# Summing expert outputs into tokens by accumulating indirect reads, and ending the last expert in its own rows

## The chip, the cores and the metric

The kernel runs on one core of one Trainium2 chip. The metric is the device time of one execution in microseconds (us). The engines are called as the profile calls them: PE (TensorE), PEld (its weight loads), DVE (VectorE), ACT (ScalarE), POOL (GpSimd) and SP (SyncE, which issues DMAs). Indirect DMAs, which gather or scatter rows by a column of indices, are issued by POOL.

## The reference

A two-layer encoder over 512 tokens of 1024 features in float32. Layer 0 is neighbourhood attention and a dense SwiGLU, layer 1 is multi-head latent attention and a top-2-of-8 expert SwiGLU; a final RMS norm follows. The change touches the part from the experts on:

```python
def _moe(h, w_router, w_gu, w_down):
    hf = h.reshape(B * S, D)
    probs = jax.nn.softmax((hf @ w_router).astype(jnp.float32), axis=-1)
    vals, idx = lax.top_k(probs, TOP_K)
    wts = vals / jnp.sum(vals, axis=-1, keepdims=True)
    combine = jnp.sum(jax.nn.one_hot(idx, N_EXPERTS, dtype=jnp.float32) * wts[..., None], axis=1)
    y = jnp.zeros_like(hf)
    for e in range(N_EXPERTS):
        y = y + combine[:, e:e + 1] * _swiglu(hf, w_gu[e], w_down[e])
    ...
x = x + g_f[:, None, :] * f      # f is the result of _moe, g_f one row of 1024 gates
return _rmsnorm(x) * final_norm
```

So every token gets two expert rows, each times a weight of its own, the sum times a gate row `g_f`, and is then normalised over its 1024 features.

## The kernel before

Float32 products are made in three passes: each operand is split into a high part (`hi`, cast on ACT, L195) and a rest (`lo`, subtracted on DVE, every sixth piece on POOL, L198), and PE adds hi·hi, hi·lo and lo·hi (L1245 to L1247). A weight tile goes by SP's queue from HBM into a raw slot (L168), is split into one of a few hi/lo slots, and is used by PE. The raw slots are a ring: `N_RAWX` = 3 of a pool for this phase, two in `big_raw`, three of `rawp`; SP issues in order and waits for the next slot of the ring to be split.

The experts are walked in 88 steps, 11 for each expert (`steps`, L1396): steps 0 to 6 are gate and up (256 columns of each), 7 and 8 the left half of the down product, 9 and 10 the right half. One step takes two weight tiles ("jobs"). The order of all instructions is as written (`manual_schedule`). The split of a step's weights is written two steps ahead: `emit_to(2 * i + PRE)` opens step i, `emit_to(2 * i + POST)` closes it, and what a step writes between the two stands on ACT and DVE ahead of the split of step i + 2. An expert handles its first 128 rows always; a second block of up to 128 rows is under a branch on the expert's count (`second_block`, L1382), in a narrow form for at most 64 rows (`few`). In the profiled execution the last expert (number 7) takes the second block, so its gate steps are twice as long.

Tokens that chose an expert are gathered by an indirect read of `HT` into `xb0` and `xb1`. A finished expert's rows leave PSUM by an ACT copy (`out_rows`, L1271) and are written to a DRAM table `Y`, unweighted, 256 rows per expert for experts 0 to 6. While expert 7 runs, eight indirect reads of `Y` (for each of four token blocks of 128 the two chosen experts; column `dest`) go through one tile `xb1`, and DVE multiplies each by the token's weight `wm` and the gate row (L1544) and adds it to `x_tok`, the residual in token order (L1545). `x_tok` lies in `big_raw`, and comes back from the DRAM table `XT` at the beginning of expert 7.

Expert 7's own rows don't go by DRAM. They are weighted on DVE (`weigh`), split, and put into token order by PE with a one-hot matrix `oh` (`last_rows`, L1607 to L1617): 16 products of 512 columns for the left half, twice 16 of 256 for the right one. DVE adds each to `x_tok`, ACT sums the squares (L1623). The right half's down product is made in two pieces of 256 columns, for each of the two row blocks. When all is summed, `final_rstd` makes the reciprocal root and DVE scales eight pieces, each stored as it is done (L1604, L1605). `overflow` handles an expert with more than 256 rows; its branch isn't taken.

Of the kernel before, what the change touches and what calls it, by code (L numbers as in the profile page):

```python
# [19 lines left out]
P = 128  # L20
# [20 lines left out]
N_RAWX = 3  # L41
# [17 lines left out]
class Kernel:  # L59
    def __init__(self, ctx, tc, d, dbg=None):  # L60
# [8 lines left out]
        self.Y = self.dram.tile([(NE - 1) * CAP, D], F32, name="Y")  # L69
# [698 lines left out]
    def ffn_phase(self, xT, hH, hL, norm):  # L768
        nc, tc = self.nc, self.tc
        with ExitStack() as es:  # L770
# [17 lines left out]
            for g, (f0, f1) in enumerate(self.ffn_groups()):  # L788
# [201 lines left out]
    def router(self, small, hp, ps_a, ps_b, ps_c, cst):  # L990
# [64 lines left out]
        def rest(R, C, T, idx0, ps_y):  # L1055
# [33 lines left out]
            dest, wm, near = small("dest", 8, dt=I32), small("wm", 8), small("near", 8)  # L1089
# [23 lines left out]
            for n in range(8):  # L1113
                nc.tensor.matmul(ps[:, 32:34], R[:, n].bitcast(F32), W[:, n], start=n == 0, stop=n == 7)
            tab, idx, w_row = small("tab", 32), small("idx", 32, dt=I32), small("w_row", 2)
            V.tensor_scalar(tab, ps[:, 0:32], -1.0, None, op0=OP.add)
            V.tensor_scalar(idx, tab, 0.0, None, op0=OP.max)
            V.tensor_copy(w_row, ps[:, 32:34])
# [6 lines left out]
            self.rt = dict(idx=idx, tab=tab, dest=dest, wm=wm, w=w, r=r, col=col, w_row=w_row)  # L1125
# [4 lines left out]
    def moe_phase(self, xT, oH, oL):  # L1130
        nc, tc, d = self.nc, self.tc, self.d
        with ExitStack() as es:
# [66 lines left out]
            xb1 = st.tile([P, D], F32, name="xb1")  # L1199
            act1 = st.tile([P, 256], F32, name="act1")  # L1200
# [101 lines left out]
            def few_out(e, n, ps):  # L1302
                gs = w2.tile([P, S], F32, name="yo")[0:FEW]
                nc.scalar.copy(gs, ps[FEW:P])
                nc.vector.tensor_add(gs, ps[0:FEW], gs)
                r0 = e * CAP + P
                nc.gpsimd.dma_start(Y[r0:r0 + FEW, n * S:(n + 1) * S], gs)

            def overflow():

                iota, tokid = cst[:, 0:128], cst[:, 128:132]
                with tc.tile_pool(name="over", bufs=1, side="right") as op:
                    C = op.tile([P, 32], F32, name="C")
                    tab2 = [op.tile([P, 2, NE, 2], F32, name=f"tab2{i}") for i in range(2)]
# [60 lines left out]
                for i in range(4):  # L1375
                    for n in range(3):
                        self.square_sum(x_tok, w2, ssq, n, i)
# [57 lines left out]
            ssq = st.tile([P, 6, 4], F32, name="ssq")  # L1435
# [7 lines left out]
            def weigh(cols, ps, b=0):  # L1443

                for b, p in enumerate(ps, b):
                    t = w2.tile([P, S], F32, name="yo")[:, cols]
                    nc.vector.scalar_tensor_tensor(t, p[:, cols], self.rt["w_row"][:, b:b + 1], gf_row[:, n * S:(n + 1) * S][:, cols], op0=OP.mult, op1=OP.mult)  # L1447
                    self.split_piece(yl[:, n, b, 0, cols], yl[:, n, b, 1, cols], t)

            last = NE - 1  # L1450
            for i, (e, s) in enumerate(steps):
# [16 lines left out]
                parts = [ALL] if e < last or s < 9 else HALVES if s == 9 else HALVES[0:1]  # L1468
# [8 lines left out]
                else:  # L1477
                    if g == 0:
                        pys = [ps_y.tile([P, S], F32, name="y", tag="y") for _ in parts]
                        py = pys[0]  # L1480
# [250 lines left out]
```

## Time and profile before

| what | before |
|---|---|
| device time, median of 3 (lowest to highest) | 1646.16 us (1645.68 to 1646.4) |
| profiled execution, its own device time | 1649.19 us |
| its span, first to last instruction | 1647.3 us |
| mean granted clock of TensorE | 0.989 |
| busy share of the span: PE, PEld, DVE, ACT, POOL | 95%, 76%, 67%, 50%, 19% |
| DMA queue of SP, share of 16 engines' span | 54.0% |

The experts begin at about 935 us. PE is busy nearly all the time: of 20 us it works 18 to 20 in every stretch from 960 to 1620 us. From 1300 to 1480 us the DMA engines are also full (share 0.96 to 1.08). The last expert runs from about 1503 us to the end, and after 1620 us the work thins out: a few PE products, DVE and ACT in turn, then the stores.

A row of a timeline reads: start in us, length in us, engine, line of the code, operation, what is written from what, shape, how many; and in brackets how long the engine was idle before it and whose end it waited for.

### The profile page before, as it was taken

The numbers are of one execution on the slowest core, as the hardware profiler recorded it, in microseconds if no ns is written. First come the engines' busy times: TensorE is split into PE (matmuls) and PEld (weight loads), VectorE is DVE, ScalarE is ACT, GpSimd is POOL, SyncE is SP. The second block draws the span as 40 slices with busy tenths as digits, with TensorE's granted clock in tenths as the row PEclk, the third lists the DMA queues.
The fourth block names the chain that finished last, engine by engine and source line by source line (L and its number), as shares of the span: only waits on it lengthen the run. The fifth ranks groups of instructions, "written<-read, shape, count | busy, mean of one in ns | idle before, by whom it ended". The sixth has DMA issues, their size and how long they took to land. (4 is left out here: it accounts for less than half of the span.)

```text
span 1647.3 us, 23092 instructions
## 1 busy us (share of the span) xinstructions
PE 1572.5 (95%) x7909; PEld 1245.2 (76%) x7909; DVE 1107.1 (67%) x1688; ACT 819.9 (50%) x1384; POOL 310.9 (19%) x259
## 2 busy tenths in 40 slices
PE   6899999999999999989999989999999999999996
PEld 4677779888888888856668677778887777777885
DVE  4687855765655434698865668656447888887765
ACT  3455544422222123577663656545436677765442
POOL 0332310002000000021101343112123324233310
PEclk9999999999999999999999989999999999999998
DMA  9545533467544523222112599758568999997751
GB/s 355 186 141 166 169 119 103 146 216 253 194 160 158 193 77 112 74 77 77 52 65 69 182 360 355 256 187 259 175 192 295 334 351 357 345 371 260 262 192 53
DMA packets 241209, 327.38 MB, mean 199 GB/s; under 512 B 9586, under 2 KB 191570, under 8 KB 240404
## 3 DMA queue, kind: packets, MB, share of 16 engines
q1 hardware_dynamic: 231072, 296.19, 54.0%
q0 software_dynamic: 5232, 18.09, 3.0%
q10 hardware_dynamic: 4740, 11.02, 1.8%
q8 instruction: 89, 1.46, 0.4%
q14 instruction: 76, 0.62, 0.1%
HBM read 308.75 MB, written 16.52 MB: 197 GB/s over the span
## 5 line engine op out<-in xcount | busy, mean ns | idle before, releaser
L198 DVE TENSOR_TENSOR lo<-raw,hi 128x1024 fp32r<-128x1024 f32 (+1 forms) x284 | 374.9, 1350 | 92.4 <-ACT hi L195 84.8
L195 ACT CAST hi<-raw 128x1024 fp32r<-128x1024 f32 (+1 forms) x319 | 318.3, 1045 | 225.0 <-PE mm L296 146.3
L296 PE MATMUL mm<-hL,hi 128*128 128x512 f32 x480 | 190.7, 397 | 0.0
L295 PE MATMUL mm<-hH,hi 128*128 128x512 f32 x480 | 190.1, 396 | 0.1
L297 PE MATMUL mm<-hH,lo 128*128 128x512 f32 x480 | 190.1, 396 | 0.0
L1245 PE MATMUL gu<-hi,he 128*128 128x512 f32 x360 | 144.5, 401 | 9.6 <-ACT act L1255 3.9
L198 POOL TENSOR_TENSOR lo<-raw,hi 128x1024 fp32r<-128x1024 f32 x39 | 101.6, 2606 | 236.1 <-ACT hi L195 187.0
L1247 PE MATMUL gu<-hi,he 128*128 128x512 f32 x360 | 141.2, 392 | 0.0
L1246 PE MATMUL gu<-lo,he 128*128 128x512 f32 x360 | 140.8, 391 | 0.0
L225 DVE SCALAR_TENSOR_TENSOR ada_acc<-raw,c_act,ada_acc 128x1024 f32<-128x1024 f32 x70 | 90.4, 1291 | 31.9 <-DMA raw<-in_w_ada_dram 31.3
L295 PEld LDWEIGHTS mm<-hH,hi 128*128 128x128 f32 x480 | 90.4, 188 | 20.9 <-ACT hi L195 0.5
L296 PEld LDWEIGHTS mm<-hL,hi 128*128 128x128 f32 x480 | 90.3, 188 | 19.9 <-issue 1.0
L297 PEld LDWEIGHTS mm<-hH,lo 128*128 128x128 f32 x480 | 90.4, 188 | 19.2 <-issue 0.2
L1245 PEld LDWEIGHTS gu<-hi,he 128*128 128x128 f32 x360 | 67.6, 188 | 30.6 <-issue 7.8
L1255 ACT ACTIVATE act<-gu 128x256 f32<-128x256 f32 x56 | 21.5, 384 | 138.8 <-PE gu L1247 138.8
L198 DVE TENSOR_TENSOR lo<-raws,hi 128x1024 fp32r<-128x1024 f32 x50 | 73.4, 1501 | 14.6 <-ACT hi L195 12.9
L1245 PE MATMUL y<-hi,a 128*128 128x512 f32 (+1 forms) x200 | 77.5, 387 | 2.2 <-PEq L1384 1.7
L1247 PEld LDWEIGHTS gu<-hi,he 128*128 128x128 f32 x360 | 67.6, 188 | 15.5 <-DVE he L209 0.4
L326 POOL TENSOR_TENSOR rs<-rs 128x2 f32<-128x2 f32 (+1 forms) x8 | 2.7, 336 | 402.4 <-DVE rs L324 402.4
L1246 PEld LDWEIGHTS gu<-lo,he 128*128 128x128 f32 x360 | 67.6, 188 | 13.2
L1247 PE MATMUL y<-hi,a 128*128 128x512 f32 (+1 forms) x200 | 75.4, 377 | 0.0
L1246 PE MATMUL y<-lo,a 128*128 128x512 f32 (+1 forms) x200 | 75.3, 376 | 0.0
(399 smaller groups left out, 3642.4 us busy)
## 6 DMA issues: line engine op xcount, KB each, us to landing
raw<-in_moe_w_gu_dram SPq DMA_DIRECT2D x176, 512.0 KB
raw<-in_w_ada_dram SPq DMA_DIRECT2D x48, 1024.0 KB
raw<-in_moe_w_down_dram SPq DMA_DIRECT2D x37, 1024.0 KB
raws<-in_moe_w_gu_dram SPq DMA_DIRECT2D x48, 512.0 KB
raw<-in_ffn_w_gu_dram SPq DMA_DIRECT2D x22, 1024.0 KB
raw<-in_na_w_qkv_dram SPq DMA_DIRECT2D x12, 1024.0 KB
raws<-in_moe_w_down_dram SPq DMA_DIRECT2D x11, 1024.0 KB
raw<-in_ffn_w_down_dram SPq DMA_DIRECT2D x8, 1024.0 KB
```

The costliest lines, as they stand in the source:

```text
L195: nc.scalar.copy(hi[:, c], raw[:, c])
L198: eng.tensor_tensor(lo[:, c], raw[:, c], hi[:, c].bitcast(F32), op=OP.subtract)
L225: nc.vector.scalar_tensor_tensor(acc, raw[:, i], c, acc, op0=OP.mult, op1=OP.add)
L295: nc.tensor.matmul(ps, ah, bh, start=first, stop=False)
L296: nc.tensor.matmul(ps, ah, bl, start=False, stop=False)
L297: nc.tensor.matmul(ps, al, bh, start=False, stop=last)
L326: g.tensor_tensor(w, y, y, op=OP.mult)
L1245: nc.tensor.matmul(ps, xh, wh, start=first, stop=False)
L1246: nc.tensor.matmul(ps, xh, wl, start=False, stop=False)
L1247: nc.tensor.matmul(ps, xl, wh, start=False, stop=last)
L1255: nc.scalar.activation(a, ps[:, 0:256], AF.Silu)
```

## The change

- A weight for every row of every expert is made in the router (`W` and `w_row` grow from 2 to 32 columns); DVE multiplies a row by its weight and the gate row as it leaves PSUM (`weigh`), where ACT copied it before. `gf_row` is loaded at step 3 of expert 0.
- `Y` gets one more row, of zeros; a token whose chosen expert is 7, or whose place is beyond 256, reads that row.
- In expert 7, steps 1 to 4, eight indirect reads with an add (`compute_op=OP.add`) go straight into `x_tok`; DVE does nothing for them.
- At step 6 the summed tokens are stored to `XT` again, and ACT sums their squares (`token_sums`). At step 7 expert 7's rows of `XT` are gathered into `xr`. At step 8 the left half of expert 7's result is added to them (`rows_add`), and all tokens are normalised (`tokens_norm`); at step 9 SP stores them all to the output.
- Step 9 leaves out the second block; step 10 makes it whole, in two pieces of 256 columns of 14 k-tiles each. Each block of expert 7's rows is normalised by itself (`rows_out`) and scattered over the output by an indirect write. One-hot products, split of the result and `last_rows` are gone.
- `N_RAWX` goes from 3 to 2; in expert 7 POOL takes no part in the split (`pool_every` = 0); the register load of the largest count moves from the end to step 0 of expert 7.

The scheduler's part is small here, since the order is as written. Two engines at two places follow; a buffer's number stands only where rows would read alike. First DVE in the last expert at step 8, from its branches to the `lo` of step 10's weights (`hilo` is the split result, `raws` is `x_tok`, `second_8134` the second block's sum), before:

```order
L1384 COMPARE_AND_BRANCH
L1384 UNCONDITIONAL_BRANCH x2
L1544 SCALAR_TENSOR_TENSOR xb_8143<-xb_8143,wm,gf_row 128x1024
L1545 TENSOR_TENSOR raws<-raws,xb_8143 128x1024
L1447 SCALAR_TENSOR_TENSOR yo<-y,w_row,gf_row 128x512
L209 TENSOR_TENSOR hilo<-yo,hilo 128x512
L1447 SCALAR_TENSOR_TENSOR yo<-second_8134,w_row,gf_row 128x512
L209 TENSOR_TENSOR hilo<-yo,hilo 128x512
L198 TENSOR_TENSOR lo<-raw,hi 128x1024 x2
```

The same place on DVE after (`second_8136` is the second block's sum):

```order
L1491 SCALAR_TENSOR_TENSOR yo<-y,w_row,gf_row 128x512
L1492 TENSOR_TENSOR xr<-xr,yo 128x512
L1491 SCALAR_TENSOR_TENSOR yo<-second_8136,w_row,gf_row 128x512
L1492 TENSOR_TENSOR xr<-xr,yo 128x512
L1614 TENSOR_TENSOR xg<-xr,fn_row 128x512 x2
L1459 SCALAR_TENSOR_TENSOR ssq<-ssq 128x4
L1463 RECIPROCAL ssq<-ssq 128x4
L1464 SCALAR_TENSOR_TENSOR ssq<-ssq 128x4
L1465 TENSOR_TENSOR ssq<-ssq 128x4
L1466 SCALAR_TENSOR_TENSOR ssq<-ssq 128x4
L1481 SCALAR_TENSOR_TENSOR raws<-raws,ssq,fn_row 128x1024 x4
L198 TENSOR_TENSOR lo<-raw,hi 128x1024 x3
```

The `lo` of step 10 stood behind two weightings and two splits of the result, one of its three pieces on POOL; now all three stand behind the additions to `xr`, the root of the tokens' sums and four scalings of 1024 columns. Between the rows L1459 and L1463 ACT takes the root: on ACT two sums of squares (L1470), a table load and the root (L1462) stand ahead of the casts of step 10's weights.

Then PE near the end, from the first block's last products (`y`) into the second block's (`second`), before:

```order
L1245 MATMUL y<-hi,a 128x256
L1246 MATMUL y<-lo,a 128x256
L1247 MATMUL y<-hi,a 128x256
L1614 MATMUL gu<-hilo,xb 128x256 x16
L1562 COMPARE_AND_BRANCH
L1245 MATMUL second_8134<-hi,a 128x256
L1246 MATMUL second_8134<-lo,a 128x256
```

The same place after:

```order
L1246 MATMUL y<-hi,a 128x512
L1247 MATMUL y<-lo,a 128x512
L1248 MATMUL y<-hi,a 128x512
L1624 COMPARE_AND_BRANCH
L1246 MATMUL second_8135<-hi,a 128x256
L1247 MATMUL second_8135<-lo,a 128x256
L1248 MATMUL second_8135<-hi,a 128x256
```

Before, 16 one-hot products stood between the blocks, and 16 more behind the second; after, the first block's columns come in one piece, the second block's in two (42 rows each of steps 9 and 10 together), and nothing stands behind the second.

The diff, cut to its core:

```diff
-N_RAWX = 3
+N_RAWX = 2
...
-        self.Y = self.dram.tile([(NE - 1) * CAP, D], F32, name="Y")
+        self.Y = self.dram.tile([(NE - 1) * CAP + 1, D], F32, name="Y")
...
+                    for n in range(2):
+                        nc.gpsimd.dma_start(self.Y[(NE - 1) * CAP:, n * S:(n + 1) * S], zero[0:1])
...
-            W = T[:, 256:272].rearrange("p (n c) -> p n c", n=8)
-            here = iota[:, 4 * (NE - 1):4 * (NE - 1) + 2]
+            W = T[:, 256:512].rearrange("p (n c) -> p n c", n=8)
-                nc.gpsimd.tensor_scalar(W[:, n], here, col[:, n:n + 1], w[:, n:n + 1], op0=OP.is_equal, op1=OP.mult)
+                nc.gpsimd.tensor_scalar(W[:, n], iota[:, 0:32], col[:, n:n + 1], w[:, n:n + 1], op0=OP.is_equal, op1=OP.mult)
...
-            V.scalar_tensor_tensor(wm, place, float(CAP), w, op0=OP.is_lt, op1=OP.mult)
-            V.scalar_tensor_tensor(wm, ce, NE - 1.0, wm, op0=OP.is_lt, op1=OP.mult)
-            V.tensor_scalar(near, place, CAP - 1.0, None, op0=OP.min)
+            V.tensor_scalar(near, place, float(CAP), 1e4, op0=OP.is_ge, op1=OP.mult)
+            V.tensor_add(near, near, place)
-            V.tensor_scalar(dest, near, (NE - 1.0) * CAP - 1.0, None, op0=OP.min)
+            V.tensor_scalar(dest, near, (NE - 1.0) * CAP, None, op0=OP.min)
...
+            def weigh(out, rows, e, n, b):
+
+                c = 4 * e + b
+                nc.vector.scalar_tensor_tensor(out, rows, self.rt["w_row"][0:rows.shape[0], c:c + 1],
+                                               gf_row[0:rows.shape[0], n * S:(n + 1) * S], op0=OP.mult, op1=OP.mult)
+
             def out_rows(e, n, b, ps):
                 yo = w2.tile([P, S], F32, name="yo")
-                nc.scalar.copy(yo, ps)
+                weigh(yo, ps, e, n, b)
...
+            def rstd_of(sums, v, y, z):
+
+                nc.vector.scalar_tensor_tensor(v, sums[0], EPS, sums[1], op0=OP.add, op1=OP.add)
+                for x in sums[2:]:
+                    nc.vector.tensor_add(v, v, x)
+                nc.scalar.activation(z, v, AF.Sqrt)
+                nc.vector.reciprocal(y, z)
+                nc.vector.scalar_tensor_tensor(z, y, -0.5, y, op0=OP.mult, op1=OP.mult)
+                nc.vector.tensor_mul(z, z, v)
+                nc.vector.scalar_tensor_tensor(y, z, 1.5, y, op0=OP.add, op1=OP.mult)
+
+            def square_sum(x, out):
+                t = w2.tile([P, S], F32, name="yo")[:, 0:x.shape[-1]]
+                nc.scalar.activation(t, x, AF.Square, scale=D ** -0.5, accum_out=out)
+
+            def token_sums():
+                for t in range(4):
+                    for h in range(2):
+                        square_sum(x_tok[:, t, h * S:(h + 1) * S], ssq[:, h, t:t + 1])
+
+            def tokens_norm():
+                y = ssq[:, 3]
+                rstd_of([ssq[:, 0], ssq[:, 1]], ssq[:, 2], y, ssq[:, 4])
+                for t in range(4):
+                    nc.vector.scalar_tensor_tensor(x_tok[:, t], x_tok[:, t], y[:, t:t + 1], fn_row, op0=OP.mult, op1=OP.mult)
+
+            def to_tokens(table, rows, b):
+                nc.gpsimd.indirect_dma_start(out=table, out_offset=bass.IndirectOffsetOnAxis(ap=spot[:, b:b + 1], axis=0),
+                                             in_=rows[:, b], in_offset=None, bounds_check=S - 1, oob_is_err=False)
+
+            def rows_add(b, ps, cols, c0, n=0):
+
+                c = slice(c0 + cols.start, c0 + cols.stop)
+                t = w2.tile([P, S], F32, name="yo")[:, cols]
+                nc.vector.scalar_tensor_tensor(t, ps[:, cols], self.rt["w_row"][:, 4 * last + b:4 * last + b + 1], gf_row[:, c], op0=OP.mult, op1=OP.mult)
+                nc.vector.tensor_add(xr[:, b, c], xr[:, b, c], t)
+                if n < 2:
+                    square_sum(xr[:, b, c], rss[:, b, n:n + 1])
+                else:
+                    nc.vector.tensor_tensor_reduce(t, xr[:, b, c], xr[:, b, c], op0=OP.mult, op1=OP.add, scale=1.0 / D, scalar=0.0, accum_out=rss[:, b, n:n + 1])
+
+            def rows_out(b):
+
+                rstd_of([rss[:, b, n:n + 1] for n in range(2 + b)], *(rss[:, b, n:n + 1] for n in range(3, 6)))
+                y = rss[:, b, 4:5]
+                if b:
+                    nc.scalar.mul(xg[:, 1, 0:S], xg[:, 1, 0:S], y)
+                    nc.vector.scalar_tensor_tensor(xg[:, 1, PIECES[2]], xr[:, 1, PIECES[2]], y, fn_row[:, PIECES[2]], op0=OP.mult, op1=OP.mult)
+                    nc.vector.tensor_scalar_mul(xg[:, 1, PIECES[1]], xg[:, 1, PIECES[1]], y)
+                else:
+                    nc.scalar.mul(xg[:, 0], xg[:, 0], y)
+                to_tokens(d["out"], xg, b)
 
...
+                ws_b = ws if s < 7 or g == 0 else ws_b + ws
...
-                second_block(n_reg, many, few if e < last else None)
+                if e < last or s < 9:
+                    second_block(n_reg, many, few if e < last else None)
...
+                        n_max = nc.values_load(cnt[0:1, 8:9], min_val=0, max_val=S)
...
+                        self.pool_every = 0
+                        tab_e = tab[:, 4 * last:4 * last + 2]
+                        nc.vector.tensor_scalar(spot, tab_e, 0.0, 2.0 * S, op0=OP.is_lt, op1=OP.mult)
+                        nc.vector.tensor_tensor(spot, spot, tab_e, op=OP.add)
                     if s == 5:
                         self.turn_no %= len(self.slots)
                         self.slots.remove("big")
-                    if 1 < s <= 9:
-                        c = s - 2
-                        xs = x_tok[:, c % 4]
-                        nc.vector.scalar_tensor_tensor(xb1, xb1, wm[:, c:c + 1], gf_row, op0=OP.mult, op1=OP.mult)
-                        nc.vector.tensor_add(xs, xs, xb1)
-                    if 1 <= s < 9:
-                        gather(xb1, Y, dest, s - 1)
+                    if 1 <= s < 5:
+                        for c in (2 * s - 2, 2 * s - 1):
+                            nc.gpsimd.indirect_dma_start(out=x_tok[:, c % 4], out_offset=None, in_=Y, compute_op=OP.add,
+                                                         in_offset=bass.IndirectOffsetOnAxis(ap=dest[:, c:c + 1], axis=0))
+                    if s == 6:
+                        for t in range(4):
+                            nc.scalar.dma_start(XT[t * P:(t + 1) * P], x_tok[:, t])
+                    if s == 6:
+                        token_sums()
+                    if s == 7:
+                        for b in range(2):
+                            gather(xr[:, b], XT, idx, 4 * last + b)
                     if s == 8:
-                        yl = self.big_split.rearrange("p a (b c d) -> p a b c d", b=2, c=2)
-                        nc.scalar.activation(ssq[:, 5, 0:1], self.ones[:, 0:1], AF.Sqrt)
-                    if s == 8:
-                        weigh(ALL, (py, ps1))
+                        rows_add(0, py, ALL, 0)
+                        rows_add(1, ps1, ALL, 0)
+                        for b in range(2):
+                            nc.vector.tensor_mul(xg[:, b, 0:S], xr[:, b, 0:S], fn_row[:, 0:S])
+                        tokens_norm()
                     if s == 9:
-                        self.last_rows(0, ALL, oh, yl, x_tok, ps_gu, w2, ssq)
+                        for t in range(4):
+                            nc.sync.dma_start(d["out"][t * P:(t + 1) * P], x_tok[:, t])
                     if s == 10:
-                        weigh(HALVES[0], (py, ps1))
-                        cols = HALVES[1]
-                        for t in range(2):
-                            down(pys[1], A, 0, 2 * g + t, ws[t], cols)
-                        weigh(cols, pys[1:])
-                        self.last_rows(1, HALVES[0], oh, yl, x_tok, ps_gu, w2, ssq)
-                        with tc.If(n_reg > P):
-                            for t in range(2):
-                                down(second[1], A, 1, 2 * g + t, ws[t], cols)
-                        weigh(cols, second[1:], 1)
-                        self.last_rows(2, cols, oh, yl, x_tok, ps_gu, w2, ssq)
+                        rows_add(0, py, ALL, S, 1)
+                        nc.vector.tensor_mul(xg[:, 0, S:D], xr[:, 0, S:D], fn_row[:, S:D])
+                        rows_out(0)
+                        for h in range(2):
+                            with tc.If(n_reg > P):
+                                for t in range(4):
+                                    down(second[h], A, 1, t, ws_b[t], HALVES[h])
+                            rows_add(1, second[h], HALVES[h], S, 1 + h)
+                            if h == 0:
+                                c = PIECES[1]
+                                nc.vector.tensor_mul(xg[:, 1, c], xr[:, 1, c], fn_row[:, c])
+                        rows_out(1)
...
+                if i == 3:
+                    nc.scalar.dma_start(gf_row, self.GF.broadcast_to([P, D]))
...
-            with tc.If(n_max > CAP) as many_rows:
+            with tc.If(n_max > CAP):
-            for i in range(4):
-                for h in range(2):
-                    c = slice(h * S, (h + 1) * S)
-                    nc.vector.scalar_tensor_tensor(x_tok[:, i, c], x_tok[:, i, c], y[:, i:i + 1], fn_row[:, c], op0=OP.mult, op1=OP.mult)
-                    (nc.sync if h else nc.scalar).dma_start(d["out"][i * P:(i + 1) * P, c], x_tok[:, i, c])
...
```

## Rows read from the trace of the kernel before

**Rows 1.** The page's first line: span of the profiled execution.
```profile
span 1647.3 us, 23092 instructions
```

**Rows 2.** Stretch of expert 5: length, busy PE, PEld, DVE, ACT, POOL, clock, DMA share, GB/s.
```profile
1360.00:1380.00 20.00, 18.16 (x79) 14.10 (x78) 17.98 (x15) 15.57 (x19) 7.89 (x5) 1.00 1.08 352
```

**Rows 3.** Timeline of PE from step 8 of expert 7 to its end.
```profile
1595.40 0.48 PE L1245 MATMUL y<-hi,a 128*128 128x512 f32 x1
...
1603.67 0.28 PE L1245 MATMUL y<-hi,a 128*128 128x256 f32 x1
...
1615.17 4.00 PE L1614 MATMUL gu<-hilo,xb 128*128 128x512 f32 x16
...
1630.51 0.28 PE L1247 MATMUL second<-hi,a 128*128 128x256 f32 x1
```

**Rows 4.** Timeline of DVE in the same stretch.
```profile
1599.16 1.28 DVE L1544 SCALAR_TENSOR_TENSOR xb<-xb,wm,gf_row 128x1024 f32<-128x1024 f32 x1
1600.47 1.23 DVE L1545 TENSOR_TENSOR raws<-raws,xb 128x1024 f32<-128x1024 f32 x1
...
1603.88 0.75 DVE L1447 SCALAR_TENSOR_TENSOR yo<-second,w_row,gf_row 128x512 f32<-128x512 f32 x1
...
1630.90 0.48 DVE L1447 SCALAR_TENSOR_TENSOR yo<-second,w_row,gf_row 128x256 f32<-128x256 f32 x1 [1.80 <-PE second L1247]
...
1635.43 0.16 DVE L1588 SCALAR_TENSOR_TENSOR ssq<-ssq 128x4 f32<-128x4 f32 x1 [0.53 <-DVE raws L1616]
...
1636.99 5.39 DVE L1604 SCALAR_TENSOR_TENSOR raws<-raws,ssq,fn_row 128x512 f32<-128x512 f32 x8
```

**Rows 5.** Timeline of ACT in expert 7: the table load, a sum of squares.
```profile
1597.75 1.28 ACT L1550 ACT_TABLE_LOAD   x1
...
1617.07 0.63 ACT L1623 ACTIVATE yo<-raws 128x512 f32<-128x512 f32 x1 [8.94 <-issue]
```

**Rows 6.** Indirect reads of POOL's queue: count, median us from issue to landing.
```profile
xb<-HT,idx POOLq DMA_INDIRECT x11, 8.2
...
xb<-Y,dest POOLq DMA_INDIRECT x8, 5.0
```

**Rows 7.** Two stretches of expert 0, columns as in Rows 2.
```profile
951.00:953.00 2.00, 0.43 (x2) 0.43 (x2) 0.67 (x1) 0.00 (x0) 2.00 (x4) 0.71 1.04 311
...
961.00:963.00 2.00, 2.00 (x8) 1.64 (x7) 0.00 (x0) 0.00 (x0) 1.61 (x2) 0.73 1.09 348
```

**Rows 8.** Timeline of PE: router products, starts in experts 4 and 6.
```profile
952.57 0.64 PE L1112 MATMUL y<-a 128*128 128x32 f32 x2 [3.06 <-POOL a L1107]
...
1304.82 0.47 PE L1245 MATMUL gu<-hi,he 128*128 128x512 f32 x1 [0.30 <-PEq L1384]
...
1443.82 0.47 PE L1245 MATMUL gu<-hilo,he 128*128 128x512 f32 x1 [1.12 <-ACT act L1255]
```

**Rows 9.** Register loads of an expert's count on PE.
```profile
L1380 PEldq TENSOR_LOAD <-cnt x8: 306/315/493, 925.3 to 1442.9; - x8
```

**Rows 10.** Timeline of POOL in the router's part.
```profile
936.44 3.52 POOL L1108 TENSOR_SCALAR yo<-cst,col,w 128x2 f32<-128x2 f32 x1
...
953.44 0.48 POOL L1107 TENSOR_SCALAR a<-cst,col 128x32 fp32r<-128x32 f32 x1
953.90 0.38 POOL L1108 TENSOR_SCALAR yo<-cst,col,w 128x2 f32<-128x2 f32 x1
```

**Rows 11.** Timeline of ACT at the casts for expert 4's first step.
```profile
1298.47 2.00 ACT L195 CAST hi<-raws 128x1024 fp32r<-128x1024 f32 x2 [0.60 <-DMA raw<-in_moe_w_gu_dram]
```

**Rows 12.** Timeline of DVE: the last `lo` of that step's weights.
```profile
1305.93 1.21 DVE L198 TENSOR_TENSOR hilo<-raw,hilo 128x1024 fp32r<-128x1024 f32 x1
```

**Rows 13.** ACT's DMA issues of XT at the end of the first steps of expert 0.
```profile
941.92 1.91 ACTq L1577 DMA_DIRECT2D XT<-raws  x2
```

**Rows 14.** The same stretch, SP's queue: the issue that waited for XT's landing.
```profile
946.91 1.04 SPq L168 DMA_DIRECT2D raws<-in_moe_w_gu_dram  x2
```

**Rows 15.** POOL's issues of indirect reads: ns shortest, median, longest.
```profile
L1206 POOL DMA_INDIRECT xb<-Y,dest x8: 939/1684/1814, 1520.9 to 1602.0; - x8
```

More of the change, by code (lines that the diff above doesn't have):

```diff
@@ L1088, in rest @@
             w = chosen("w", bc(pw, 1, 2))
-            dest, wm, near = small("dest", 8, dt=I32), small("wm", 8), small("near", 8)
+            dest, near = small("dest", 8, dt=I32), small("near", 8)
             q, r, col = small("q", 8), small("r", 8), small("col", 8)
@@ L1467, in moe_phase @@
                     ps1 = second[0]
-                parts = [ALL] if e < last or s < 9 else HALVES if s == 9 else HALVES[0:1]
+                ws_b = ws if s < 7 or g == 0 else ws_b + ws
                 if s < 7:
@@ L1478, in moe_phase @@
                     if g == 0:
-                        pys = [ps_y.tile([P, S], F32, name="y", tag="y") for _ in parts]
-                        py = pys[0]
-                    for b, cols in enumerate(parts):
-                        for t in range(2):
-                            down(pys[b], A, 0, 2 * g + t, ws[t], cols)
+                        py = ps_y.tile([P, S], F32, name="y", tag="y")
+                    for t in range(2):
+                        down(py, A, 0, 2 * g + t, ws[t])
                     flush()
@@ L1498, in many @@
                     if s >= 7:
-                        for ps, cols in zip(second, parts):
-                            for t in range(2):
-                                down(ps, A, 1, 2 * g + t, ws[t], cols)
+                        for t in range(2):
+                            down(ps1, A, 1, 2 * g + t, ws[t])
                     if prev is not None:
@@ L1553, in moe_phase @@
                     if s == 9:
-                        self.last_rows(0, ALL, oh, yl, x_tok, ps_gu, w2, ssq)
+                        for t in range(4):
+                            nc.sync.dma_start(d["out"][t * P:(t + 1) * P], x_tok[:, t])
                     if s == 10:
-                        weigh(HALVES[0], (py, ps1))
-                        cols = HALVES[1]
-                        for t in range(2):
-                            down(pys[1], A, 0, 2 * g + t, ws[t], cols)
-                        weigh(cols, pys[1:])
@@ new lines, in moe_phase @@
+                        rows_out(0)
+                        for h in range(2):
+                            with tc.If(n_reg > P):
+                                for t in range(4):
+                                    down(second[h], A, 1, t, ws_b[t], HALVES[h])
[3 more added lines that the diff above has]
+                                nc.vector.tensor_mul(xg[:, 1, c], xr[:, 1, c], fn_row[:, c])
@@ L1596, in moe_phase @@
-            with tc.If(n_max > CAP) as many_rows:
-                overflow()
-                final_rstd()
-            with many_rows.Else():
-                final_rstd()
-            for i in range(4):
-                for h in range(2):
-                    c = slice(h * S, (h + 1) * S)
-                    nc.vector.scalar_tensor_tensor(x_tok[:, i, c], x_tok[:, i, c], y[:, i:i + 1], fn_row[:, c], op0=OP.mult, op1=OP.mult)
-                    (nc.sync if h else nc.scalar).dma_start(d["out"][i * P:(i + 1) * P, c], x_tok[:, i, c])
@@ L1607, in last_rows @@
-    def last_rows(self, piece, cols, oh, yl, x_tok, ps_gu, w2, ssq):
-        nc = self.nc
-        for i in range(4):
-            ps = ps_gu.tile([P, S], F32, name="gu", tag="gu")[:, cols]
-            for b in range(2):
-                for z in range(2):
-                    nc.tensor.matmul(ps, oh[:, b, i * P:(i + 1) * P], yl[:, piece > 0, b, z, cols], start=b == 0 and z == 0, stop=b == 1 and z == 1)
-            xs = x_tok[:, i, PIECES[piece]]
-            nc.vector.tensor_add(xs, xs, ps)
-            self.square_sum(x_tok, w2, ssq, piece, i)
```

54 lines of the change are left out of this document (17 added, 37 removed).

## Prediction

> **What bounds the kernel now.** I read the profiled execution's length first [rows 1]: 1647.3 us of span, 1649.19 us of device time, 3.03 us over the median of 1646.16; differences are worked out in the span and set onto the median. Then the stretches of 20 us in the experts [rows 2]: PE is busy 18.16 of 20 us, DVE 17.98, and the DMA engines are full at 352 GB/s. So PE's order decides until the last expert's end, with DVE and the DMA engines close behind it, and what DVE or SP gets in addition has little room. Last I read PE and DVE over the end of the last expert [rows 3, 4]. The last down matmul starts at 1630.51, and from there to the end of the span 16.8 us pass: weighting, split, one-hot products, sums, a root, eight scalings (5.39 us in one row) and the stores. The end is a single chain, and every term below is a change of that chain or of PE's work ahead of it.
>
> **What goes (A, B).** Up to step 9's start at 1603.67 PE's work in the last expert is the same. From there, before, 26.8 us pass to the last down matmul, one-hot products among them (16 of 512 columns take 4.0 us, [rows 3]), and the right half of the first block is made in halves. After, the first block has 24 products of 512 columns in step 9 and 18 in step 10, then the second block 84 of 256. Step 8's 36 products of 512 take 1595.40 to 1603.67, 0.23 us each; step 9's 96 of 256 take 1603.67 to 1615.17, 0.12 each. So 1603.67 + 42 x 0.23 + 84 x 0.12 = 1623.4 for the last one if nothing waits: A = -7.1 us.
>
> Behind the last matmul, after: its end 0.39 (1630.51 to DVE's 1630.90), the weighting of 256 columns 0.48 [rows 4], an add of 256 that I put at 0.40 (1.23 for 1024 columns) and the sum of squares on DVE, which no row shows: 0.4 as another add, 1.0 as a row of twice the width, taken 0.55, near the first. The root is seven small steps, 1635.43 to 1636.99, 1.56. The last scaling is another 0.48, and 0.65 goes to the hops between engines (0.53 stands in the root's row alone). That is 4.5. Then POOL issues the scatter, 0.94 as the shortest of the indirect reads, 1.8 the longest [rows 15], and it lands. No row shows a scatter; the indirect reads of the same size land after 5.0 and those of HT after 8.2 [rows 6]. I take 5.0, since its rows too are 128 rows of 4 KB: 10.4 us in place of 16.8, B = -6.4 (bounds -2.3 with 8.2 and 1.8, and -6.9 with the sum of squares and the hops at their least).
>
> **What comes in at the end (C, D, E).** The order of DVE shows the three `lo` pieces of step 10's weights behind all that step 8 adds. The second block's sum is done when step 9 starts, so the chain begins at 1603.88 as in the row of the weighting. It goes: weighting 0.75, add about 0.63; then ACT needs a sum of squares of 512 (0.63 and 0.19 to read it), the table load 1.28 and a root 0.2 [rows 5], while DVE makes two products; four small steps 0.8; four scalings of 1024 columns, 1.31 from start to start by 1599.16 and 1600.47, 5.2; one `lo` of 1.2. The sum is 1603.88 + 1.38 + 2.3 + 0.8 + 5.2 + 1.2 = 1614.8, with the hops 1614.9. PE has step 9's 24 products done at 1609.2 and, with the second block gone from that step, nothing else to do: it stands from 1609.4. C = +5.5. Below is 4, where the first products need only `hi` and the second and third piece come faster than PE uses them; above is 8, where the scatter of small steps repeats for the first block (its own root stands on DVE and ACT ahead of the second block's rows).
>
> A PE that stood still gets a lower clock here. PE stood for 3.06 us up to 952.57 [rows 8]; the granted clock is 0.71 of full in 951 to 953 and still 0.73 in 961 to 963 [rows 7], means over a fall to the lower level, 1.2 of 2.4 GHz, and over the rise out of it at about 962.1. So up to 9.5 us of PE's work ran at the lower level, which loses half its length: at most 4.7. In the new stall PE still makes the products that need no `lo`, so I take 5.6 us of work at the lower level, D = +2.8 (0 if the clock stays).
>
> The register load of the largest count now stands in the last expert's first step. On PE such a load takes 0.32 us [rows 9], but the stretch that holds it in expert 6 has PE idle for 1.12 (row of 1443.82, [rows 8]): E = +1.1 (0.3 to 1.2).
>
> **What changes on the way (F, G).** F: POOL's eight products `W` grow from 2 to 32 columns; their neighbours of 32 take 0.48 for 0.38 [rows 10], so +0.8 for eight, and PE waits for POOL there (3.06 us in its row of 952.57, [rows 8]). One row of 2 columns took 3.52. A rule of the Trainium skill bears on that row ("SBUF — State Buffer", section "Who interferes with whom"): GpSimd reading SBUF and a DVE instruction with two SBUF inputs shut each other out for the whole instruction. By it a longer `W` meets DVE more often, and F would be nearer +2; the trace agrees in that single row and no other. I keep +0.8 (0, or 3.9 with one more row as long as that).
>
> G: the raw ring has seven slots for eight. The DMA engines are full there, so SP has one slot less to be early by; 1 MB at 352 GB/s is 3.0 us. In expert 4 the casts already wait 0.60 for a transfer [rows 11], the last `lo` of that step ends at 1307.1 [rows 12], and PE starts the step at 1304.82 [rows 8] and, at 0.23 us a product, comes to that last piece not before 1307.6 to 1309, so up to 2 us are to spare. DVE also takes the weighting of 0.75 where ACT copied, twice to four times per expert, in that stretch. If the transfers keep their mean rate the ring costs nothing; if they are late by a whole slot at each of four experts it is 12. I take +1.0, near the first.
>
> Nothing else is on the path. The adding reads are issued in steps 1 to 4, two per step from about 1521 (the first plain read's issue, [rows 15]), and even two in turn per token block are landed near 1579 with one POOL issue of 1.8 and 5.0 each. A rule of the Trainium skill ("Collectives: The Full Stack", section "The bandwidth ceiling: the fold count and why AG ≠ RS ≠ AR") says that a transfer that adds reads two sources for one write. By it the 5.0 us of a read would be about 10, an estimate; eight of them are still landed by 1579, and no run here shows an adding read. The store of the sums and their gather follow: the store of the same 2 MB of XT kept SP waiting from 941.92 to 946.91 [rows 13, 14], so the gather at step 7 goes out at about 1586 and lands 8 us later, 1594, for an addition that starts after 1599. DVE loses sixteen rows of 1.3 us in those steps [rows 4] and gets POOL's `lo` pieces for them. Behind the sums of squares on ACT, 8 x 0.82 = 6.6 us [rows 5], stand the casts of step 8's weights; PE needs these at 1595.40, with some 4 us to spare.
>
> **The sum.** -7.1 - 6.4 + 5.5 + 2.8 + 1.1 + 0.8 + 1.0 = -2.3 us, so 1643.9 us from 1646.16.
>
> **The rivals.** First, faster: the stall is smaller and the clock stays: C = 4, D = 0, G = 0, E = 1.1, F = 0.8 and the -13.5 of A and B: -7.6, and with 0.7 kept for the second and third `lo` -6.9, 1639.3 us. For it speaks that PE's first products of step 10 need `hi` only, so that it isn't idle throughout; against it that all three `lo` are behind the scalings.
>
> Second, slower: the ring. A slot less makes the first steps of experts 3 to 7 late, because the DMA engines are full in that stretch, each late start costing up to one slot, 3.0 us. The other terms sum to -3.3; so from 3.3 us in all, a little over one slot, the gain is gone, and from 6.6, over two, it is slower by more than can be told. Three late starts make 9.0, 1651.9 us, and four 1654.9; I put it at 1651.9. For it speaks the 0.60 us of waiting in [rows 11] and DVE's 90% [rows 2]; against it that a wait of that size stands inside 2 us of slack.
>
> Third, the new chain is late: sums, XT store, gather of rows. If the adding reads take twice their time and the store cannot start before 1590, the gather lands at 1604 to 1606 and the additions on DVE, with everything behind them, shift by about 5: -2.3 + 5 = +2.7, 1648.9. The slack of 5 us between 1594 and 1599 speaks against it.
>
> **How the numbers follow.** The forecast has 0.50, with an own range of 1640 to 1648 (C from 4 to 8, D from 0 to 4.7, not all at one end); the faster rival 0.22, the ring 0.17, the late chain 0.11. Less than 0.2%, 3.3 us, can't be told from no change. Faster by more: the faster rival and 0.19 of the forecast, 0.41. Slower by more: 0.14 of the ring, 0.05 of the late chain and 0.06 of the forecast, 0.25. Between them 0.34. The range of 1637 to 1652 reaches from the faster rival with a scatter somewhat quicker than a read to three late starts of the ring; four of them, and a slow scatter on top of a late chain, are left out.
>
> **What would show it.** In the profile after: PE idle for 4 to 6 us ahead of step 10's first `lo` product, with DVE's four scalings of 1024 columns right before that `lo`, and a granted clock of about 0.5 behind it (C, D); 10.4 us from the start of the last down matmul to the end of the span (B); ACT's casts at the starts of experts 3 to 6 with DMA waits no longer than 0.6 (G); no wait of DVE for `xr` (third rival). The forecast is wrong if PE doesn't stand there, if it stands at the experts' starts, or if the tail is 13 us or more.

## The result, and the profile after

The changed kernel is slower: a median of 1662.13 us (1657.47 to 1664.38) against 1646.18, a ratio of 1.0098 (95% interval 1.0085 to 1.0112), so about 16 us. The forecast was 1643.9. The profiled execution, at 1664.38 us the longest of the six, has this span [rows 1]:

```profile
span 1662.5 us, 22851 instructions
```

Where the 15.2 us of span came in is read by following the same work on PE in both traces:

| place on PE | before | after | after less before |
|---|---|---|---|
| start of expert 4 (gate, first product) | 1304.82 | 1302.85 | -2.0 |
| expert 7, transposes of its first block | 1498.31 | 1498.22 | -0.1 |
| expert 7, first product after an idle time | 1504.09 | 1505.84 | +1.8 |
| first product of step 9 | 1603.67 | 1624.12 | +20.5 |
| last down product | 1630.51 | 1650.88 | +20.4 |
| end | 1647.3 | 1662.5 | +15.2 |

Nearly all of it lies inside the last expert, between 1506 and 1624. The row of PE that holds it, with the two other waits at the start of this expert and in it (idle time and releaser in brackets):

```profile
1500.77 0.63 PE L1216 MATMUL second<-ident,xb 128*128 128x128 f32 x4 [1.93 <-DVEq L1397]
...
1556.15 0.47 PE L1261 MATMUL tp<-ident,act 128*128 128x128 f32 x1 [16.47 <-DVE act L1257]
...
1635.02 0.80 PE L1247 MATMUL y<-lo,a 128*128 128x512 f32 x1 [4.97 <-DVE lo L198]
```

PE stood for 16.47 us. DVE, named as the releaser, had nothing to do either. The chain of waits says what the whole kernel waited for: one transfer of weights, issued at 1523.30, that took 28.60 us.

```profile
1523.30 28.60 DMA raw<-in_moe_w_gu_dram
```

The stretches show why (length, busy PE, PEld, DVE, ACT, POOL, clock, DMA share, GB/s; the second row is of the stall):

```profile
1528.00:1540.00 12.00, 11.69 (x53) 9.20 (x51) 2.36 (x2) 2.00 (x2) 7.21 (x5) 1.00 1.06 225
...
1544.00:1552.00 8.00, 0.00 (x0) 0.00 (x0) 0.00 (x0) 0.00 (x0) 0.00 (x0) 0.50 1.06 253
1554.00:1560.00 6.00, 3.85 (x10) 3.13 (x11) 6.00 (x9) 5.08 (x9) 0.00 (x0) 0.50 0.88 274
```

The DMA engines are full (1.06) and move only 225 GB/s, where they moved 352 at the same share in [rows 2]. In that time POOL's eight adding reads run. The first and the last of them go out at

```profile
1521.39 1.88 POOL L1600 DMA_INDIRECT raws<-Y,dest  x1 [12.07 <-DMA raw<-in_moe_w_gu_dram]
...
1539.92 1.55 POOL L1600 DMA_INDIRECT raws<-Y,dest  x1 [1.35 <-DMA raws<-Y,dest]
```

Written as two per step over four steps, all eight are issued within 18.5 us, while PE is in steps 1 and 2. Before, each read of `Y` waited for DVE to free the one tile they went through, and the eight were spread from 1520.9 to 1602.0 [rows 15]. SP's queue and the view of DMA issues (KB each, median us to landing) show the other side:

```profile
1525.52 14.43 SPq L168 DMA_DIRECT2D raw<-in_moe_w_gu_dram  x2
...
1540.07 8.56 SPq L168 DMA_DIRECT2D raw<-in_moe_w_gu_dram  x1
```

```profile
raws<-Y,dest POOLq DMA_INDIRECT x8, 11.5
...
out_dram<-xg,spot POOLq DMA_INDIRECT x2, 3.6
```

An adding read lands after 11.5 us where a plain one took 5.0 [rows 6], and SP is held inside the issue of a transfer for 14.4 us in two issues and 8.6 in another, where the issue ahead of the transfer in the chain above took 0.37. The weights land late, and the next ones are issued late as well; then PE comes back at the lower clock (0.50 above), and loses some 2 us more.

The trace before shows how full this stretch was without the adds:

```profile
1520.00:1540.00 20.00, 20.00 (x93) 16.22 (x92) 15.33 (x17) 10.67 (x18) 6.75 (x4) 1.00 0.90 298
```

In the run act_copy below the profiled execution took 3799.9 us, and its trace isn't read.

### The profile page after: what moved, and what is told of

It reads as the page before. It is cut to its first block, busy times and chain, and to the rows that moved or that the text cites. A ratio compares the mean times of both kernels' runs of the same rounds, so it can differ in the third digit from the quotient of the medians.

```text
span 1662.5 us, 22851 instructions
## 1 busy us (share of the span) xinstructions
PE 1567.4 (94%) x7819; PEld 1236.5 (74%) x7819; DVE 1098.0 (66%) x1689; ACT 813.1 (49%) x1365; POOL 304.8 (18%) x259
## 5 line engine op out<-in xcount | busy, mean ns | idle before, releaser
L198 DVE TENSOR_TENSOR lo<-raw,hi 128x1024 fp32r<-128x1024 f32 (+1 forms) x285 | 371.0, 1334 | 112.1 <-ACT hi L195 105.7
L195 ACT CAST hi<-raw 128x1024 fp32r<-128x1024 f32 (+1 forms) x313 | 311.6, 1044 | 252.0 <-PE mm L296 146.5
L198 POOL TENSOR_TENSOR lo<-raw,hi 128x1024 fp32r<-128x1024 f32 x32 | 88.0, 2752 | 186.8 <-ACT hi L195 155.4
L198 DVE TENSOR_TENSOR lo<-raws,hi 128x1024 fp32r<-128x1024 f32 x54 | 76.1, 1444 | 20.2 <-ACT hi L195 16.6
L1247 PE MATMUL y<-lo,a 128*128 128x512 f32 x186 | 74.7, 402 | 5.0 <-DVE lo L198 5.0
L1246 PE MATMUL y<-hi,a 128*128 128x512 f32 x186 | 76.3, 410 | 2.2 <-PEq L1397 1.8
L1248 PE MATMUL y<-hi,a 128*128 128x512 f32 x186 | 74.1, 398 | 0.0
```

The costliest lines, as they stand in the source:

```text
L195: nc.scalar.copy(hi[:, c], raw[:, c])
L198: eng.tensor_tensor(lo[:, c], raw[:, c], hi[:, c].bitcast(F32), op=OP.subtract)
L1246: nc.tensor.matmul(ps, xh, wh, start=first, stop=False)
L1247: nc.tensor.matmul(ps, xh, wl, start=False, stop=False)
L1248: nc.tensor.matmul(ps, xl, wh, start=False, stop=last)
```

## The experiments

Theory 1: the add itself makes the reads hold the DMA engines, and the weights starve. Theory 2: the burst of two reads per step does it, whatever they do. Theory 3: the weights are late because the raw ring restarts at the last expert (hardly a transfer from 1500 to 1508.8). Ratios are to the kernel before, with their 95% interval.

| run | median us | ratio | PE's stall in steps 1 to 3 of expert 7 | at step 10 |
|---|---|---|---|---|
| changed kernel | 1662.13 | 1.0098 (1.0085 to 1.0112) | 16.47 | 4.97 |
| plain_reads | 1651.36 | 1.0037 (1.0023 to 1.0051) | 2.22 | 4.97 |
| half_adds | 1653.62 | 1.0054 (1.0037 to 1.0071) | 4.89 | 4.98 |
| no_reads | 1646.35 | 1.0010 (1.0001 to 1.0019) | none | 4.99 |
| late_norm | 1655.21 | 1.0072 (1.0052 to 1.0092) | 9.09 | none |
| dve_add | 1647.18 | 1.0010 (1.0000 to 1.0020) | 1.42 | 4.97 |
| add_late | 1638.70 | 0.9961 (0.9947 to 0.9976) | 0.44 + 0.91 | none |
| reads_later | 1638.22 | 0.9962 (0.9950 to 0.9975) | none | none |
| act_copy | 1632.94 | 0.9922 (0.9907 to 0.9938) | not read | not read |
| act_scale | 1634.01 | 0.9927 (0.9914 to 0.9940) | 2.06 | none |
| act_scale_nmax | 1635.91 | 0.9947 (0.9935 to 0.9959) | 2.29 | none |
| before_ring7 | 1642.92 | 0.9990 (0.9981 to 0.9999) | (kernel before) | (kernel before) |

**plain_reads.** 

```diff
-in_=Y, compute_op=OP.add,
+in_=Y,
```

> The eight indirect reads of the last expert stay where they are, two per step in steps 1 to 4, but replace instead of add (the tokens' sums are then incomplete). Theory 1 (the add is what holds the DMA engines and with them SP's issues of the weights): the reads take half their time or less, SP's issues are back under 2 us, PE's stall of 16.47 us in the last expert shrinks to 0 to 3 us, and the lower clock behind it goes: 1644 us (1642 to 1648) for 1662. Theory 2 (the burst of two reads per step, whatever they do, starves the weights): a stall of 10 us or more, 1655 to 1662. Theory 3 (the weights are late because the ring restarts at the last expert's beginning, 1498 to 1509 without a transfer): the stall stays at 16, 1662.

The same rows in the same burst (1522.18 to 1535.74), without the add: the stall falls from 16.47 to 2.22 us, and the same stretch, columns as above, now moves

```profile
1528.00:1540.00 12.00, 12.00 (x56) 9.73 (x55) 2.46 (x3) 3.17 (x4) 4.95 (x5) 1.00 1.05 389
```

389 GB/s at the share at which the adding reads moved 225. The reads land after 7.3 us for 11.5. Theory 2 falls as the main cause: its stall of 10 us or more isn't there. Theory 1 isn't met in full either: SP's longest issue is 4.4 us, not under 2, and the median is 7 us above its 1644, outside its range.

How long the DMA engines are held can be read from the pages, in the row of POOL's queue (packets, MB, share of 16 engines' span): changed kernel, plain_reads, no_reads.

```profile
q0 software_dynamic: 5872, 20.05, 3.9%
q0 software_dynamic: 5872, 20.05, 3.3%
q0 software_dynamic: 4720, 15.86, 2.6%
```

Times the spans of 1662.5, 1648.1 and 1641.4 us these are 64.8, 54.4 and 42.7 us of all engines: some 22 us for the eight adding reads and 12 for the same reads without the add, each good to 1 or 2 us by the rounding of the shares. So the add nearly doubles the time that a read holds the engines.

**half_adds.**

```diff
-                        for c in (2 * s - 2, 2 * s - 1):
+                        for c in (s - 1,):
```

> Only four of the eight adding reads, one per step in steps 1 to 4 (the second expert of each token is left out). Theory 1: the adding reads took some 28 us of all DMA engines for eight, so four take 14 us and the weights lose half as much, 14 us less; PE had 13 us of lead before the stall, so the stall is 0 to 5 us: 1643 to 1649. Theory 2 (the pair per step): as good as none left, 1643. Theory 3: 16 us of stall, 1662.

```profile
1528.00:1540.00 12.00, 12.00 (x55) 9.73 (x54) 3.71 (x6) 2.00 (x2) 3.75 (x3) 1.00 1.05 234
...
1547.57 0.48 PE L1261 MATMUL tp<-ident,act 128*128 128x128 f32 x1 [4.89 <-DVE act L1257]
```

While the adds run the rate is as low as with eight (234), but for half the time. The stall of 4.89 us is within what theory 1 gave; the time, 1653.62, is above its range. The run says nothing on theory 2, since the edit didn't space the reads: POOL issued the four in one burst of 6.7 us,

```profile
1524.15 2.33 POOL L1600 DMA_INDIRECT raws<-Y,dest  x1 [13.46 <-DMA raws<-XT]
...
1530.82 1.54 POOL L1600 DMA_INDIRECT raws<-Y,dest  x1 [0.30 <-issue]
```

No run spreads adding reads over the expert as the plain ones were spread before, so whether spaced adds would fit stays open.

**no_reads.** The four lines with the reads are left out.

> The changed kernel without the eight adding reads (the sums then hold no expert of 0 to 6). Theory 1 (the adds hold the DMA engines): no stall in the last expert before step 10, and 1642 to 1649 us, at most 3 us less than plain_reads. Theory 3 (the ring's restart alone makes the weights late): a stall of 2 us or more stays.

No stall is left before step 10, so the ring's restart alone doesn't stop PE, and theory 3 falls as the sole cause. plain_reads is 1651.36 - 1646.35 = 5.0 us slower by the medians, more than the 3 expected. Its trace shows 2.22 us of stall for the burst, and besides a granted clock of 0.81 from 1500 to 1508.8, ahead of the reads, where the trace of no_reads has 1.00; so not all of the 5.0 is shown to be the burst's. By the medians the eight adding reads cost 15.8 us, 10.8 of them for the add.

What the restart adds to the adds isn't separated. In the trace before, the transfers pause at the last expert's start from 1496 to 1500 (DMA share 0.02), in the changed kernel from 1500 to 1510 (0.01), with PE's transposes at nearly the same time. before_ring7, which differs from the kernel before in one raw slot alone, pauses from 1492 to 1502 (0.01). So the seven-slot ring goes with a pause some 6 us longer, and with it the weights would have less lead when the adding reads come. No run has the adding reads with eight slots, so how much of the 16.47 us is the ring's isn't shown.

**late_norm.**

```diff
                         for b in range(2):
                             nc.vector.tensor_mul(xg[:, b, 0:S], xr[:, b, 0:S], fn_row[:, 0:S])
-                        tokens_norm()
...
                 emit_to(2 * i + POST)
+                if e == last and s == 8:
+                    tokens_norm()
```

> Only the place of the tokens' normalisation changes: its root and four scalings are written behind the split of step 10's weights instead of ahead of it. Theory: PE's stall of 4.97 us before step 10 was the wait for the lo pieces behind these scalings, and the 5 to 7 us at half clock behind it cost 2 more; both go: -7.0, 1655 us. Rival: the scalings now stand ahead of the additions of the first block's rows and of the scatter, and the end is as late as before: 1660 to 1662.

1655.21, as expected, and no wait of PE is left at step 10. The place was right. Of this run's gain a part may belong to the stall by the reads, which is 9.09 us in its trace; what makes that stall differ between executions (times go from 1650.9 to 1659.83) stays open.

**dve_add, add_late, reads_later.** The sums in another way, then with late_norm's edit as well, then a step later:

```diff
+                        land = [xr[:, 0], xr[:, 1], xg[:, 0], xg[:, 1]]
...
+                        if s > 1:
+                            for c in (2 * s - 4, 2 * s - 3):
+                                nc.vector.tensor_add(x_tok[:, c % 4], x_tok[:, c % 4], land[c % 4])
                         for c in (2 * s - 2, 2 * s - 1):
-                            nc.gpsimd.indirect_dma_start(out=x_tok[:, c % 4], out_offset=None, in_=Y, compute_op=OP.add,
-                                                         in_offset=bass.IndirectOffsetOnAxis(ap=dest[:, c:c + 1], axis=0))
+                            gather(land[c % 4], Y, dest, c)
```

> The same sums in another way: the reads are plain ones into four buffers that are free until step 7, two per step in steps 1 to 4, and DVE adds each to the token's row one step later, without a weight (eight adds of 1.23 us). Theory 1: DVE has room in those steps (8 to 15 of 20 us busy), the stall goes, 1644 us (1642 to 1648), as with the plain reads alone. Theory 2: the stall stays at 10 us or more. Rival for the gain: the adds stand ahead of the lo pieces of the weights on DVE and PE waits there instead, some 2.5 us per step in steps 2 to 5, 1650 or more.

> Both edits together: plain reads with eight adds on DVE, and the tokens' normalisation behind the split of step 10. Theory: the stall by the reads (16.47 us, 1.42 left with the plain reads) and the stall at step 10 (4.97 us and 2 us of lower clock behind it) are separate, so their gains add: 1647.2 - 7 = 1640.2 us, 0.997 of the kernel before. Rival: the scalings delay the first block's scatter and take back 3 to 5 us, 1644 to 1645.

> As add_late, with the eight plain reads one step later (steps 2 to 5; the last adds at step 6, ahead of the store of the sums). Theory: what is left of the stall (1.42 us) comes from reads that meet the weights just after the ring's restart at the last expert; a step later the weights have more lead, and the stall goes: 1 to 2 us less than add_late. Rival: the gather of the rows now lands after 1600 and DVE waits for it at step 8, 3 us or more above add_late.

With the adds on DVE the same sums cost 15 us less than in the changed kernel (1647.18), and DVE's eight adds don't become a wait. The reads are also spaced here: four go out from 1511.8 to 1515.6, and four from 1541.0 to 1551.1, behind DVE's adds, so the run changes the burst as well as the add. Both edits together give 1638.70, 8.5 us less again: the two stalls are separate. reads_later has no stall at all in those steps, but is no quicker (1638.22). It doesn't test its theory: its first four reads go out 16.1 us behind PE's first transposes of the expert, where in add_late it is 16.0, and only the last four are later (51.6 us for 45.2). What the last 1.4 us of stall come from stays open.

**act_copy, act_scale.** In add_late's experts:

```diff
                 yo = w2.tile([P, S], F32, name="yo")
-                weigh(yo, ps, e, n, b)
+                nc.scalar.copy(yo, ps)
```

and in act_scale, with the gate row as eight products in the last expert (the narrow form of the second block likewise keeps the weight and leaves out the gate row),

```diff
-                weigh(yo, ps, e, n, b)
+                nc.scalar.mul(yo, ps, self.rt["w_row"][:, 4 * e + b:4 * e + b + 1])
...
+                                nc.vector.tensor_mul(land[c % 4], land[c % 4], gf_row)
                                 nc.vector.tensor_add(x_tok[:, c % 4], x_tok[:, c % 4], land[c % 4])
```

> As add_late, but the rows of experts 0 to 6 leave PSUM unweighted by an ACT copy, as before the change (their weights are left out; few_out keeps its own). Theory: the 1.9 us that PE waits for a second block at the last expert's beginning, and the 2 us lost over experts 4 to 6, come from the weighting on DVE, so 3 to 4 us less than add_late. Rival: these are the register load of the largest count (1.1 us expected by the prediction) and the ring of seven slots; then the same time as add_late within 1 us, and the wait stays.

> As add_late, whole sums: the rows of experts 0 to 6 are multiplied by their weight on ACT as they leave PSUM (a scale of one number per row, in the place of the copy before the change), and the gate row is multiplied in the last expert, on DVE, eight products of 1024 columns ahead of the eight adds. Theory (the weighting on DVE made the experts' starts late): act_copy's gain comes again, less some of it for the eight products of 1.3 us: 1633 to 1636 us, and the wait of 1.93 us of PE for the second block at the last expert is gone. Rival (act_copy was quicker for another reason): 1638 to 1640 us and the wait stays.

act_copy takes 1632.94, 5.8 us less than add_late, more than the 3 to 4 expected. act_scale does the whole work in 1634.01. The same row of PE in add_late and in act_scale:

```profile
1501.49 0.30 PE L1216 MATMUL second<-ident,xb 128*128 128x128 f32 x1 [1.93 <-DVEq L1397]
```

```profile
1493.95 0.30 PE L1216 MATMUL second<-ident,xb 128*128 128x128 f32 x1 [0.18 <-DVEq L1397]
```

PE waited there for DVE to reach the branch in which the second block is weighted. With ACT doing it, the wait is 0.18. It is one wait of several: from 935 to 1502 us PE's waits for DVE, leaving aside one of 0.5 that both have, sum to 5.9 us in add_late and to 0.2 in act_scale; the largest is 2.3, at the second block of another expert. This version beats both kernels: 0.9927 of the kernel before.

**act_scale_nmax, before_ring7.** The register load back behind the last expert; and the kernel before with

```diff
-N_RAWX = 3
+N_RAWX = 2
```

> act_scale with the register load of the largest count back behind the last expert. The prediction's term E was +1.1 us for the load inside the expert. Theory: it costs nothing there, since PE's only wait at that place was for DVE: the same time within 1 us. Rival: 1.1 us less, or more than that where the load now stands in the tail.

> The kernel before with N_RAWX = 2: seven raw slots for eight, nothing else. The prediction's term for it was +1.0 us (0 to 12). Theory: the seventh slot is enough, 0 to +1 us. Rival: the first steps of experts 3 to 7 come late by up to 3.0 us each, +6 or more.

With the load at the end the kernel is 1.9 us slower by the medians, outside the 1 us of the theory, though the intervals overlap; so the load inside the expert gives no loss that can be seen. In the kernel before a raw slot less costs nothing either: 0.9990.

## Why the prediction was wrong

**The failed step** is "Nothing else is on the path". The prediction asked of the adding reads only whether they land in time for the store of the sums (they did: the last is issued at 1539.92, long before 1579). It priced them by when they land, and didn't ask what they take from the weights meanwhile. The weights of the next steps go through the same DMA engines, and in the stretch from 1520 to 1540 before the change these were already 0.90 busy. It also took "two per step" for the pace of the reads; with no work of DVE between them POOL issued all eight in 18.5 us. (Its 1579 can't be redone from the figures beside it, eight times 6.8 us from 1521 makes 1575; nothing hangs on that.) 16.47 us of stall and about 2 of lower clock are as much as the 18.2 us between the forecast and the median, in an execution 2.2 us above the median.

**The rule that was weighed** pointed there. The Trainium skill ("Collectives: The Full Stack", section "The bandwidth ceiling: the fold count and why AG ≠ RS ≠ AR") has the add of a collective read two sources where a copy reads one. By it, as an estimate, an adding read would take twice the engines' time; the traces agree, nearly in size: some 22 against 12 us of all engines for the eight, 225 against 389 GB/s at the same share, 11.5 against 7.3 us to landing. The prediction used the rule for the landing of the reads, not for the engines they hold.

**A held.** From step 9's first product to the last down product 26.76 us pass after, 26.84 before. Of the 26.76, 4.97 are the stall, 19.74 the products as counted, and the rest, 2.05, the lower clock.

**C and D held.** The stall is 4.97 for 5.5 expected, at the place named, with the four scalings ahead of the `lo` on DVE; products were spaced 0.43 behind it:

```profile
1628.96 4.87 DVE L1481 SCALAR_TENSOR_TENSOR raws<-raws,ssq,fn_row 128x1024 f32<-128x1024 f32 x4
1633.75 3.49 DVE L198 TENSOR_TENSOR lo<-raw,hi 128x1024 fp32r<-128x1024 f32 x3
```

```profile
1632.00:1638.00 6.00, 2.98 (x7) 2.40 (x8) 5.24 (x5) 0.00 (x0) 0.00 (x0) 0.54 0.72 291
```

D is 2.05 for 2.8. add_late is 8.5 us under dve_add, 7.0 by these two, which had been the expectation.

**B was near.** 11.62 us from the last down product to the end, for 10.4 expected and 16.8 before. The work up to the scatter's issue took 4.60 for 4.5, the row of the issue stands at

```profile
1655.48 0.99 POOL L1484 DMA_INDIRECT out_dram<-xg,spot  x1 [8.27 <-ACTq L1651]
```

and 6.0 us follow it, for 5.0. The two scatters land after 3.6 by the median; the trace shows no instruction and no transfer in the last 2.4. The issue took 0.99; the prediction had taken the shortest of [rows 15], 0.94, where the median is 1.68, and gave no reason, so that this piece came out is luck.

**E was mis-sized and misplaced.** The load shows no cost; PE's 1.93 us at that place are a wait for DVE's weighting. The row that the price was taken from names ACT's `act`, not the load, as what PE waited for [rows 8].

**G named the wrong cause.** The ring alone costs nothing (before_ring7); what its longer pause adds to the adding reads is open. The weighting on DVE, which the prediction named beside it within the same 1.0 us, costs 4.7 to 5.8 us in add_late against act_scale and act_copy.

**F** had the right price (0.46 us a row of 32 columns for 0.38), but PE's wait there is 0.24 us after where it was 3.06 [rows 8]; in the kernel before with seven slots it is 0.71 and 0.99. That wait varies from one execution to the next, and is no gain shown of the change; the 2.0 us by which expert 4 starts early in the table above may be of it. The prediction's "that single row and no other" is misread: in the trace before, five more rows of POOL between 939.9 and 952 are long (1.20 to 2.73 us, their like 0.47 to 0.62), and each overlaps a `lo` of DVE (L198), as the row of 3.52 does.

The faster rival and the ring were wrong; the late chain was looked for behind the reads, at the store, and the lateness came in beside them, at the weights.

## What to carry to other kernels

A transfer that is done in time for its own reader may still be the most expensive thing in the stretch: ask which other transfers share its engines, and how full these are, and price it in engine time, not in landing time. Ask too what paced the transfers before: a read that no longer waits for an engine can go out at once with all the others, whatever step it is written in. Eight adds moved from DVE into transfers were dearer here than eight adds of DVE, which had room. And an operation moved from ACT to DVE cost what PE then waited for DVE, 4.7 us in all, not its 0.75 us a time.

## What was not expected of the hardware

SP's issues of plain transfers took 14.4 us for two and 8.6 for one while the adding reads ran, and up to 4.4 for one in plain_reads, against 0.37: here the lateness began on the issuing queue, not only at the landing. Full engines alone don't give that: from 1300 to 1480 us before the change, at a DMA share of 1.05, SP's longest issue took 3.7 us. An indirect write of 512 KB landed after 3.6 us by the view of issues, less than the medians of the indirect reads [rows 6].
